# Half of the first feed-forward layer by seven block products for eight, in a two-layer decoder trunk on one core

## The chip, the cores and the metric

The kernel runs on one core of one Trainium2 chip. The metric is the device time of one execution in microseconds (us), the median of three runs. The engines are TensorE (PE, with its weight loads as PEld), VectorE (DVE), ScalarE (ACT), GpSimd (POOL) and SyncE (SP, whose queue issues nearly all transfers).

## The reference

One sequence of 1024 tokens with 1024 features passes a convolution layer and an attention layer; each is followed by a feed-forward layer (FFN) with squared ReLU and by a gated per-layer embedding (PLE).

```python
def reference(x, p, ...):
    h = x
    for i in range(DEPTH):                       # 2
        hn = rmsnorm(h, mix_norm[i])
        if i < N_A_LAYERS:                       # layer 0: GLU, 31 taps, layernorm, SiLU, pw2
            h = h + conformer_conv(hn, ...)
        else:                                    # layer 1: 16 heads, forget gates, w_o
            k, v, c_bhs = shared_kv(h, kv_norm, w_kvf, b_f)
            h = h + fox_attention(hn, attn_w_q[0], attn_w_o[0], k, v, c_bhs)
        hn = rmsnorm(h, ffn_norm[i])
        h = h + jnp.square(jax.nn.relu(hn @ ffn_w1[i])) @ ffn_w2[i]     # 1024 -> 4096 -> 1024
        gate = jax.nn.sigmoid(rmsnorm(h, ple_norm[i]) @ ple_w_gate[i])
        h = h + gate * (p[i] @ ple_w_proj[i])
    return rmsnorm(h, final_norm)
```

## The kernel before

The residual stream lies transposed in SBUF, features on partitions: `hT[0]` and `hT[1]` hold 512 tokens each ("half 0" and "half 1"), as 8 tiles of 128x512. All dense products run as three fp32r matmuls for one of float32: weights and tokens are each split into a rounded high part and the rest (`split`: ACT casts `h`, DVE or POOL subtracts to get `l`), and `mm3` issues high x high, high x low and low x high.

**A panel.** `linear` walks over weight panels of 128x1024 (512 KB). `panel` allots `raw`, loads it (line 120), casts it to `wh` on ACT (line 111) and subtracts to `wl` on DVE, or on POOL for half 0 (line 112). There are three buffers each of `wh` and `wl`, and `raws` of `raw` (2 in the first layer's pools, 1 during attention, 2 in the last pools of the output product). A panel is 24 matmuls of 128x512 (8 k-tiles by 3); `evac` then drains the PSUM bank on DVE.

**First layer** (`first`). After the GLU products DVE computes the taps of half 0 (`yA`) and then of half 1 (`yB`, 8 x 31 operations). Under the taps of half 1, PE runs `pw2` and the whole FFN of half 0 (`ffn`, four chunks of 8 inner tiles: `fa` panels, then `fb` panels; chunk c and panel j of half h are named `fa0hcj` and `fb0hcj`). `ln_silu(yB, 1)` (tiles `acc_m1`, `cs_m1`, `acc_ln1`, `st_ln1`, `bc_ln1`, `x1h1`, `x1l1`) gives the operand of half 1's `pw2`. Then come half 1's FFN and `ple` (panels `gt`). A Tile scheduler orders every engine's queue by program order, priorities and buffers; the order is fixed when the kernel is built.

**Second FFN** (`ffn_both`). Here tokens (two halves) and weights (halves of 4 k-tiles) are treated as 2x2 blocks, and `seven` forms the 2x2 block product by seven products for eight, in the order 1, 2, 5, 6, 3, 7, 4. The token operands are sums and differences of normalised halves (`z0f`, `z1f`; split operands `xf1` to `xf7`); `tokens_first` makes products 1 and 2's, which need half 0 alone, `tokens_rest` the others. `weight` makes the weight operands (`wt`, `wa`) from raw blocks `rwa`. `ffn_in` (PSUM tiles `psa`) writes the activations' seven combinations to DRAM (`rd`), and `ffn_out` (`psb`) reads them back as `rx`. The output product `out_product` before it (`wo`, eight panels of 5 k-tiles per half, then eight of 3; panel j of half h is `wo0jh` or `wo5jh`) ends with half 1's eight 3-tile panels in pools of their own; there `tokens_first` is called ahead of it.

## Time and profile before

| | |
|---|---|
| Time, median of 3 runs | 2612.85 us (2611.65 to 2614.08) |
| The profiled execution | 2616.24 us, span of the trace 2614.5 us |
| PE busy | 2457.6 us, 94% of the span |
| DVE busy | 1778.6 us, 68% |
| ACT busy | 1078.3 us, 41% |
| POOL busy | 913.1 us, 35% |
| DMA moved | 278.14 MB |

Busy PE time includes matmuls at the lower clock level; the granted clock (in shares of full speed) stands beside the busy time of a stretch. The mean clock over the execution was 0.969. Names of tiles are those of the program, and L137 is line 137 of the kernel before; in the changed kernel all lines stand 4 or more further down.

### The profile page before, as it was taken

To read this page: it belongs to the slowest core of one execution; us is meant where nothing else is said; L and a number is where in the kernel's file an instruction comes from. 1 tells how busy PE (TensorE), PEld (TensorE's weight loads), DVE (VectorE), ACT (ScalarE), POOL (GpSimd) and SP (SyncE) were. 2 spreads that over 40 slices of the span, in tenths; PEclk is the share of its full clock that TensorE was granted. 3 is DMA by queue.
4 is the path that set the end of the run, shared out by engine and by line. 5 is a ranking of instruction groups with operands and counts; after the bars stand their busy time and mean duration, and the time that the engine had idled before them with its cause. 6 is when DMAs were issued, how large, how long until landed. Compare 5 with 4: busy or idle time off the path is not lost.

```text
span 2614.5 us, 31465 instructions
## 1 busy us (share of the span) xinstructions
PE 2457.6 (94%) x11672; PEld 2053.1 (79%) x11672; DVE 1778.6 (68%) x2723; ACT 1078.3 (41%) x1670; POOL 913.1 (35%) x747
## 2 busy tenths in 40 slices
...
GB/s 128 49 71 183 57 78 105 97 97 98 92 89 105 97 97 93 101 83 88 62 57 50 51 49 73 107 59 167 97 208 154 141 212 267 153 145 121 36 125 113
DMA packets 101145, 278.14 MB, mean 106 GB/s; under 512 B 9840, under 2 KB 15600, under 8 KB 99584
## 3 DMA queue, kind: packets, MB, share of 16 engines
...
q14 instruction: 61, 0.50, 0.1%
...
## 4 chain that ended last, share of the span: by engine, by line
PE 76%; DVE 14%; issue 3%; ACT 3%; POOL 2%; DMA 2%; DVEq 0%; SPq 0%; POOLq 0%; ACTq 0%
PE ps_fb L137 13%; PE ps_fa L137 12%; PE psb L137 9%; PE psa L137 8%; PE ps_gt L137 7%; PE ps_wo L137 3%; PE psq L137 3%; DVE ya L332 3%; PE psv L137 3%; PE pg L137 3%; PE psk L137 3%; PE pa L137 3%; PE po L1002 2%; PE t L1032 2%; PE ps_pw L137 2%
## 5 line engine op out<-in xcount | busy, mean ns | idle before, releaser
L137 PE MATMUL psb<-rx,wb 128*128 128x512 f32 x1344 | 308.3, 392 | 5.7 <-ACT wb L111 5.7
L137 PEld LDWEIGHTS psb<-rx,wb 128*128 128x128 f32 x1344 | 254.0, 189 | 59.5 <-ACT wb L111 6.1
L137 PE MATMUL psa<-xf,wa 128*128 128x512 f32 x1200 | 281.4, 396 | 16.8 <-DVE xf L112 5.5
L332 DVE SCALAR_TENSOR_TENSOR ya<-u,wdw,ya 128x512 f32<-128x512 f32 x420 | 284.2, 747 | 0.0
L137 PEld LDWEIGHTS psa<-xf,wa 128*128 128x128 f32 x1200 | 228.4, 191 | 68.2 <-DVE xf L112 6.6
L111 ACT CAST wh_fb<-raw_fb 128x1024 fp32r<-128x1024 f32 x64 | 67.2, 1053 | 213.3 <-PE ps_fb L137 134.3
L111 ACT CAST wh_fa<-raw_fa 128x1024 fp32r<-128x1024 f32 x64 | 67.3, 1052 | 205.8 <-PE ps_fa L137 114.5
L390 DVE TENSOR_TENSOR hT<-ps_fb,hT 128x512 f32<-128x512 f32 x64 | 44.1, 689 | 147.8 <-PE ps_fb L137 147.8
L984 POOL TENSOR_SCALAR pr<-pr,sm 128x896 f32<-128x896 f32 (+7 forms) x128 | 100.0, 783 | 99.9 <-DVE sm L983 93.7
L205 POOL TENSOR_TENSOR r_g<-ms_g,mhalf 128x4 f32<-128x4 f32 x4 | 5.3, 1327 | 368.2 <-DVE ms_g L203 368.2
L112 DVE TENSOR_TENSOR pt<-t,pt 128x512 fp32r<-128x512 f32 (+1 forms) x160 | 99.2, 634 | 48.6 <-ACT pt L111 47.5
L1002 PE MATMUL po<-pt,V 128*128 128x256 f32 x640 | 121.7, 306 | 10.3 <-ACT pt L111 8.4
L112 POOL TENSOR_TENSOR wb<-rwb,wb 128x1024 fp32r<-128x1024 f32 x32 | 87.2, 2734 | 95.9 <-ACT wb L111 86.6
L982 ACT ACTIVATE pr<-pr,sm 128x896 f32<-128x896 f32 (+7 forms) x128 | 99.3, 776 | 51.9 <-DVE sm L981 35.0
L976 DVE CUSTOM_DVE_ANT_0 pr<-s,pr 128x512 f32<-128x512 f32 (+2 forms) x192 | 103.5, 551 | 22.9 <-POOL pr L963 12.8
L962 POOL TENSOR_SCALAR pr<-cb,ctok 128x896 f32<-128x896 f32 (+7 forms) x128 | 104.9, 826 | 36.1 <-PE t L1032 30.5
L384 DVE SCALAR_TENSOR_TENSOR fa<-ps_fa,bs_f 128x512 f32<-128x512 f32 x64 | 43.8, 689 | 108.4 <-PE ps_fa L137 105.0
L111 ACT CAST pt<-t 128x512 fp32r<-128x512 f32 (+1 forms) x160 | 84.0, 539 | 74.3 <-PE t L1032 70.9
L112 POOL TENSOR_TENSOR wl_fb<-raw_fb,wh_fb 128x1024 fp32r<-128x1024 f32 x32 | 77.4, 2420 | 104.0 <-ACT wh_fb L111 104.0
L112 POOL TENSOR_TENSOR wl_fa<-raw_fa,wh_fa 128x1024 fp32r<-128x1024 f32 x32 | 79.1, 2474 | 90.8 <-ACT wh_fa L111 90.8
L112 DVE TENSOR_TENSOR rx<-rx 128x1024 fp32r<-128x1024 f32 x56 | 79.9, 1437 | 41.8 <-ACT rx L111 41.8
L1002 PEld LDWEIGHTS po<-pt,V 128*128 128x128 f32 x640 | 92.8, 196 | 18.7 <-ACT pt L111 12.4
...
## 6 DMA issues: line engine op xcount, KB each, us to landing
...
rd<-e SPq DMA_DIRECT2D x112, 256.0 KB, 2.5
rx<-rd SPq DMA_DIRECT2D x28, 1024.0 KB, 5.6
...
```

The source lines that it names most:

```text
L111: copy(h, src)
L112: sub.tensor_tensor(l, src, h.bitcast(F32), ALU.subtract)
L137: self.nc.tensor.matmul(ps, p[:, k, :], q[:, k, :], start=(start and k == k0 and n == 0), stop=(stop and k == kt - 1 and n == 2), skip_gro ...
L332: nc.vector.scalar_tensor_tensor(d, s(j), w(j), o, ALU.mult, ALU.add)
L384: nc.vector.scalar_tensor_tensor(t, ps, 0.0, s[h][1], ALU.max, ALU.mult)
L390: nc.vector.tensor_tensor(hT[h][:, j, :], ps, hT[h][:, j, :], ALU.add)
L962: nc.gpsimd.tensor_scalar(z, cb[:, 0:W], -1.0, self.ctok[:, i, n : n + 1], ALU.mult, ALU.add)
L976: nc.vector.tensor_tensor_reduce(zz, ps[:, 0 : hi - lo], zz, -1.0, 3.0e38, ALU.add, ALU.min, sm[:, m : m + 1])
L982: nc.scalar.activation(z, z, AF.Exp, bias=sm[:, 0:1], scale=-1.0, accum_out=sm[:, 2:3])
L984: nc.gpsimd.tensor_scalar(z, z, sm[:, 3:4], 1.0, ALU.mult, ALU.mult)
L1002: nc.tensor.matmul(po, V[:, j, n % 4, :], pt[:, q, c : c + 256], start=(j == 0 and q == 0), stop=(jp == u and jj == 1 and q == 1),)
L1032: nc.tensor.transpose(ps[:, c : c + P], pr[b][:, j * P : (j + 1) * P], self.ident)
```

## The change

The first FFN keeps its first two chunks (16 of 32 inner tiles) as plain panels, once for each half (`PLAIN = (0, 1)`). The other 16 inner tiles are done for all tokens by `ffn_both`, two inner tiles of each weight half at a time (`pair=False`: groups `psa00` to `psa03`, then `psb00` and `psb01`). For that:

- The residual of half 0 and of half 1 is stored to DRAM twice each (`keep`, 2 MB a time): before the plain chunks (`hp`), from which the token operands are made, and after them (`hq`), to which `ffn_out` adds.
- The first pools of `first` end after half 0's plain chunks. Half 1's `ln_silu`, `pw2` and plain chunks run in new pools with one `raw` buffer: `work_pools(c1, 4, 1, 3)`.
- `tokens_first` (from `hp[0]`) and the first part of `tokens_rest` (from `hp[1]`) are called around half 1's plain chunks.
- `ple` of the first layer gets pools of its own and walks over the halves one after the other (`apart=(1, 0)`), loading its weights twice.

In the second FFN, `tokens_first` is called during the output product, ahead of half 1's first eight panels, and the last eight panels' pools have one `raw` buffer: `work_pools(c3, 2, 1, 1)`. The pools of `ffn_both` are allotted from the other side of SBUF.

```diff
+PLAIN = (0, 1)
...
-        for c in range(NCH):
+        for c in chunks:
             r = {h: self.xpair(f"r{l}{c}", h) for h in halves}
...
-            self.linear(a["wf2"][l, c], KT, r, evac2, f"fb{tag}{c}", **kw)
+            self.linear(a["wf2"][c], KT, r, evac2, f"fb{tag}{c}", **kw)
+        return s
...
-    def tokens_first(self, hT, gain, name):
-
-        hd = self.dr.tile([NH, P, KT * HB], F32, name=f"hd_{name}")
-        self.nc.sync.dma_start(hd[0], hT[0].rearrange("p k t -> p (k t)"))
-        bc = self.stats(hT, 0, name)[1]
-        f = self.slot([P, 2, 4, HB], F32, f"z0{name}")
+    def keep(self, dst, hT):
+        self.nc.sync.dma_start(dst, hT.rearrange("p k t -> p (k t)"))
+
+    def tokens_first(self, src, bc, gain, name):
+
+        f = self.slot([P, KT, HB], F32, f"z0{name}")
+        src = self.fetch(f, src)
+        f = f.rearrange("p (i k) t -> p i k t", i=2)
         x = {}
         for p, i in ((1, 0), (2, 1)):
...
+    def fetch(self, f, src):
+        if len(src.shape) == 3:
+            return src
+        self.nc.sync.dma_start(f.rearrange("p k t -> p (k t)"), src)
+        return f
...
-    def ffn_both(self, l, first):
+    def ffn_both(self, l, x, hd, t0, n, w2, rest, pair):
...
-                load(0)
-                load(1)
...
-                self.ffn_in(l, (0, 1), raw, sp, x, rd, between)
-                for g in range(2, 8):
-                    load(g)
-                    self.ffn_in(l, (g,), raw, sp, x, rd)
+                gs = [(0, 1)] if pair else [(0,)]
+                gs += [(g,) for g in range(len(gs[0]), n // 2)]
+                for i, g in enumerate(gs):
+                    for j in g:
+                        load(j)
+                    self.ffn_in(l, g, raw, sp, x, rd, None if i else between)
...
             with tc.high_priority(offset=back + 3000):
                 self.pw2(hT, x1, 0)
-                self.ffn(hT, 0, (0,), sub=nc.gpsimd)
-            self.sqp, self.sqt = self.tp, "bc"
+                self.keep(hp[0], hT[0])
+                s0 = self.ffn(hT, 0, (0,), PLAIN, sub=nc.gpsimd)[0]
+                self.keep(hq[0], hT[0])
+        with ExitStack() as c1:
+            self.work_pools(c1, 4, 1, 3)
+            self.psum_pools(c1, 4)
+            self.sqt, self.sqp = "sq", self.pool(c1, "sq0", 3)
             x1 = self.ln_silu(yB, 1)
             self.pw2(hT, x1, 1)
-            self.sqt, self.sqp = "sq", self.pool(c1, "sq0", 3)
-            self.ffn(hT, 0, (1,))
-            self.ple(hT, 0, pj0)
-        return pj1
+            self.keep(hp[1], hT[1])
+            first = self.tokens_first(hp[0], s0[1], "ffn0", "f0")
+            s1 = self.ffn(hT, 0, (1,), PLAIN)[1]
+            self.keep(hq[1], hT[1])
+            late = self.tokens_rest(*first, hp[1], s1[1])
+        hT = self.ffn_both(0, first[0], hq, KT * len(PLAIN), FF // P // 2 - 4 * len(PLAIN), self.a["wf2s0"], lambda: late, False)
+        with ExitStack() as c1:
+            self.work_pools(c1, 5)
+            self.psum_pools(c1, 5)
+            self.sqt, self.sqp = "sq", self.pool(c1, "sq5", 3)
+            self.ple(hT, 0, pj0, (1, 0))
+        return hT, pj1
...
-                if k0 == 0 and h == 0:
+                if h == 0 and k0 == 0:
                     for p in range(KSPLIT, NP - 1):
                         self.load_o(od, p)
+                elif h == 0:
+                    with tc.high_priority(offset=1):
+                        self.keep(hf[0], self.hn[0])
+                        first = self.tokens_first(self.hn[0], self.stats(self.hn, 0, "f1")[1], "ffn1", "f1")
         with ExitStack() as c3:
-            self.work_pools(c3, 2)
+            self.work_pools(c3, 2, 1, 1)
             self.psum_pools(c3, 2)
             self.sqp = None
-            first = self.tokens_first(self.hn, "ffn1", "f1")
             for _ in self.out_product(KSPLIT, NP, (1,)):
                 pass
-        return first
+        return self.hn, hf, first
```

**First place: from half 0 to half 1 in the first layer.** On PE, the last matmuls of half 0's second chunk (panel `fb0017`) were followed by the third chunk's first panel, and half 1's layer norm stood far behind, inside the fourth chunk:

```order
L137 MATMUL ps_fb0017_0_3726<-r01h0_3206,wh_fb0017_3722 128x512
L137 MATMUL ps_fb0017_0_3726<-r01l0_3207,wh_fb0017_3722 128x512
L137 MATMUL ps_fb0017_0_3726<-r01h0_3206,wl_fb0017_3723 128x512
L137 MATMUL ps_fa0020_0_3760<-f00xh0_2603,wh_fa0020_3756 128x512
L137 MATMUL ps_fa0020_0_3760<-f00xl0_2604,wh_fa0020_3756 128x512
L137 MATMUL ps_fa0020_0_3760<-f00xh0_2603,wl_fa0020_3757 128x512
```

In the changed kernel the three small groups of half 1's layer norm (`cs_m1`, `st_ln1`, `bc_ln1`) and then its `pw2` stand right behind the same panel:

```order
L141 MATMUL ps_fb0017_0_3729<-r01h0_3209,wh_fb0017_3725 128x512
L141 MATMUL ps_fb0017_0_3729<-r01l0_3210,wh_fb0017_3725 128x512
L141 MATMUL ps_fb0017_0_3729<-r01h0_3209,wl_fb0017_3726 128x512
L353 MATMUL cs_m1_3783<-acc_m1_3775,meanm_75 128x512
L193 MATMUL st_ln1_3793<-meanm_75,acc_ln1_3794 128x1 x4
L162 MATMUL bc_ln1_3825<-ident_68,r_ln1_3823 128x128 x4
L141 MATMUL ps_pw210_1_3886<-x1h1_3862,wh_pw210_3882 128x512
L141 MATMUL ps_pw211_1_3918<-x1h1_3862,wh_pw211_3914 128x512
```

The two chunks that stood between the last `fb0017` matmul and the layer norm's first matmul have gone from there, and nothing stands in their place.

**Second place: DVE in half 1's last plain chunk.** This is the part of the queue around the panels `fb0110` to `fb0113`, the evacuations of their PSUM banks into `hT1` and the splits of their weights; before:

```order
L112 TENSOR_TENSOR r01l1_5812<-fa0161_6060,r01h1_5811 128x512
L384 SCALAR_TENSOR_TENSOR fa0171_6096<-ps_fa0117_1_6071,bs_f011_5263 128x512
L112 TENSOR_TENSOR wl_fb0112_6168<-raw_fb0112_6165,wh_fb0112_6167 128x1024
L112 TENSOR_TENSOR r01l1_5812<-fa0171_6096,r01h1_5811 128x512
L390 TENSOR_TENSOR hT1_92<-ps_fb0110_1_6107,hT1_92 128x512
L112 TENSOR_TENSOR wl_fb0113_6200<-raw_fb0113_6197,wh_fb0113_6199 128x1024
L390 TENSOR_TENSOR hT1_92<-ps_fb0111_1_6139,hT1_92 128x512
L112 TENSOR_TENSOR wl_fb0114_6232<-raw_fb0114_6229,wh_fb0114_6231 128x1024
L390 TENSOR_TENSOR hT1_92<-ps_fb0112_1_6171,hT1_92 128x512
L112 TENSOR_TENSOR wl_fb0115_6264<-raw_fb0115_6261,wh_fb0115_6263 128x1024
```

In the changed kernel, the second half's normalised tokens (`z1f0`), the differences with the first half's (`z0f0`) and the split `xf05` stand between the same rows:

```order
L116 TENSOR_TENSOR r01l1_4761<-fa0171_5045,r01h1_4760 128x512
L427 SCALAR_TENSOR_TENSOR z1f0_5308<-z1f0_5308,vec_66,bs_f011_4212 128x512 x8
L394 TENSOR_TENSOR hT1_92<-ps_fb0110_1_5056,hT1_92 128x512
L441 TENSOR_TENSOR z0f0_4137<-z1f0_5308,z0f0_4137 128x1024
L116 TENSOR_TENSOR wl_fb0112_5117<-raw_fb0112_5114,wh_fb0112_5116 128x1024
L441 TENSOR_TENSOR z0f0_4137<-z1f0_5308,z0f0_4137 128x1024
L394 TENSOR_TENSOR hT1_92<-ps_fb0111_1_5088,hT1_92 128x512
L441 TENSOR_TENSOR z1f0_5308<-z1f0_5308 128x1024
L116 TENSOR_TENSOR xf05_5316<-z0f0_4137,xf05_5316 128x1024
L441 TENSOR_TENSOR z1f0_5308<-z1f0_5308 128x1024
L116 TENSOR_TENSOR xf05_5316<-z0f0_4137,xf05_5316 128x1024
L116 TENSOR_TENSOR wl_fb0113_5149<-raw_fb0113_5146,wh_fb0113_5148 128x1024
```

Eight normalisations and four differences now stand ahead of splits of `fb` panels that they don't feed.

**Third place: SP at the end of the output product.** Here the loads of the last eight panels (`raw_wo501` and on) stood behind four loads of second-FFN weights (`rwa100` to `rwa103`, 512 KB each):

```order
L120 DMA raw_wo071_14940<-in_wo 128x640
L526 DMA rwa100_15195<-in_wf1 128x2x512
L526 DMA rwa101_15196<-in_wf1 128x2x512
L526 DMA rwa102_15197<-in_wf1 128x2x512
L526 DMA rwa103_15198<-in_wf1 128x2x512
L120 DMA raw_wo501_15042<-in_wo 128x384
L120 DMA raw_wo511_15059<-in_wo 128x384
```

In the changed kernel they stand behind eight such loads and the two halves of a store of `xf12` (1 MB each, `xd_f1`), the second of which waits for the last split of `tokens_first`:

```order
L124 DMA raw_wo071_15029<-in_wo 128x640
L541 DMA rwa11_15232<-in_wf1 128x2x512 x4
L480 DMA xd_f1_15345<-xf12_14863 128x2048
L541 DMA rwa100_15224<-in_wf1 128x2x512
L541 DMA rwa101_15225<-in_wf1 128x2x512
L541 DMA rwa102_15226<-in_wf1 128x2x512
L541 DMA rwa103_15227<-in_wf1 128x2x512
L481 DMA xd_f1_15345<-xf12_14863 128x2048
L124 DMA raw_wo501_15071<-in_wo 128x384
L124 DMA raw_wo511_15088<-in_wo 128x384
```

Four loads and 2 MB of stores moved ahead of `raw_wo501`; on DVE and ACT, too, the splits of `rwa10` and `rwa11` now stand ahead of `wl_wo501`.

## Rows read from the trace of the kernel before

**Rows 1.** Page, part 1: busy us, share of the span, instructions of each engine.

```profile
PE 2457.6 (94%) x11672; PEld 2053.1 (79%) x11672; DVE 1778.6 (68%) x2723; ACT 1078.3 (41%) x1670; POOL 913.1 (35%) x747
```

**Rows 2.** Stretches: length; busy (count) PE, PEld, DVE, ACT, POOL; clock; DMA share; GB/s.

```profile
419.00:506.70 87.70, 87.70 (x388) 72.67 (x387) 69.92 (x108) 26.44 (x33) 38.41 (x16) 1.00 0.29 99
...
1079.80:1168.90 89.10, 89.10 (x401) 73.70 (x399) 48.35 (x66) 25.11 (x38) 3.12 (x2) 1.00 0.22 73
1824.80:1859.20 34.40, 17.82 (x66) 13.89 (x65) 26.59 (x29) 15.22 (x21) 3.79 (x2) 0.72 0.34 138
2160.00:2210.00 50.00, 43.95 (x180) 35.17 (x179) 44.89 (x42) 21.06 (x23) 20.70 (x8) 0.93 0.82 290
2482.20:2501.90 19.70, 14.13 (x57) 12.12 (x56) 9.15 (x14) 7.86 (x11) 2.39 (x2) 0.65 0.27 94
```

**Rows 3.** Timeline of DVE, 243 to 277: start, busy, instruction, count, idle before.

```profile
243.38 0.69 DVE L344 TENSOR_TENSOR acc_m<-y 128x512 f32<-128x512 f32 x1
...
274.25 2.29 DVE L358 SCALAR_TENSOR_TENSOR y<-y,vec,lsg 128x512 f32<-128x512 f32 x3
276.45 0.69 DVE L112 TENSOR_TENSOR x1l<-y,x1h 128x512 fp32r<-128x512 f32 x1
```

**Rows 4.** Timeline of PE, 243 to 280 us.

```profile
251.19 2.05 PE L349 MATMUL cs_m<-acc_m,meanm 128*128 128x512 f32 x2 [7.39 <-DVE acc_m L346]
...
276.31 1.65 PE L137 MATMUL ps_pw<-x1h,wh_pw 128*128 128x512 f32 x3 [7.37 <-ACT x1h L111]
```

**Rows 5.** Timeline of DVE, 484 to 513 us.

```profile
506.69 0.69 DVE L390 TENSOR_TENSOR hT<-ps_fb,hT 128x512 f32<-128x512 f32 x1 [4.75 <-PE ps_fb L137]
```

**Rows 6.** The tile raw_fb, all its instructions: ns minimum/median/maximum.

```profile
L111 ACT CAST wh_fb<-raw_fb x64: 1039/1053/1056, 360.9 to 1063.5; 128x1024 fp32r<-128x1024 f32 x64
...
L112 DVE TENSOR_TENSOR wl_fb<-raw_fb,wh_fb x32: 1224/1226/1226, 763.5 to 1064.6; 128x1024 fp32r<-128x1024 f32 x32
...
DMA to landing us min/median/max: 3.3/3.5/4.9
```

**Rows 7.** Timeline of all engines, 728.9 to 730.5 us.

```profile
728.96 1.23 DVE L112 TENSOR_TENSOR wl_fa<-raw_fa,wh_fa 128x1024 fp32r<-128x1024 f32 x1
...
730.22 0.33 SPq L120 DMA_DIRECT2D raw_fa<-in_wf  x1
```

**Rows 8.** Groups by line of DVE, 1820 to 1900: busy, mean ns.

```profile
L422 DVE SCALAR_TENSOR_TENSOR z0f<-hTb,vec,bs_f 128x512 f32<-128x512 f32 x8 | 5.4, 743 | 0.0
L112 DVE TENSOR_TENSOR wa<-rwa,wa 128x1024 fp32r<-128x1024 f32 x4 | 4.8, 1219 | 0.0
L436 DVE TENSOR_TENSOR z0f<-z1f,z0f 128x1024 f32<-128x1024 f32 x4 | 4.8, 1215 | 0.0
```

**Rows 9.** DMA issues: count, KB each, median us to landing.

```profile
hd<-hT SPq DMA_DIRECT2D x2, 2048.0 KB, 8.1
...
raw_wo<-in_wo SPq DMA_DIRECT2D x16, 192.0 KB, 2.3
...
xd_f<-xf SPq DMA_DIRECT2D x2, 1024.0 KB, 6.4
```

**Rows 10.** Timeline of PE, 1803 to 1862 us.

```profile
1804.73 0.50 PE L137 MATMUL ps_wo<-xoh,wh_wo 128*128 128x512 f32 x1 [2.16 <-ACT wh_wo L111]
...
1824.57 0.39 PE L137 MATMUL ps_wo<-xoh,wl_wo 128*128 128x512 f32 x1
...
1832.97 12.06 PE L137 MATMUL psa<-xf,wa 128*128 128x512 f32 x44 [0.76 <-DVE xf L112]
...
1859.15 3.05 PE L137 MATMUL psa<-xf,wa 128*128 128x512 f32 x9
```

**Rows 11.** The tile raw_wo, all its instructions, both widths.

```profile
L111 ACT CAST wh_wo<-raw_wo x32: 495/614/736, 1721.4 to 1817.7; 128x640 fp32r<-128x640 f32 x16, 128x384 fp32r<-128x384 f32 x16
L112 DVE TENSOR_TENSOR wl_wo<-raw_wo,wh_wo x32: 548/685/1451, 1722.1 to 1818.6; 128x640 fp32r<-128x640 f32 x16, 128x384 fp32r<-128x384 f32 x16
```

**Rows 12.** Timeline of PE, 1176 to 1197 us.

```profile
1177.63 0.82 PE L137 MATMUL psv<-wh_wv,atxh 128*128 128x272 f32 x2 [8.73 <-ACT wh_wv L111]
```

More of the change, by code (lines that the diff above doesn't have):

```diff
@@ L83, in v, with pool @@
         return self.vec[:, o + k : o + k + 1]
-    def pool(self, ctx, name, bufs, space=None):
+    def pool(self, ctx, name, bufs, space=None, side=None):
         kw = {} if space is None else {"space": space}
+        if side is not None:
+            kw["side"] = side
         return ctx.enter_context(self.tc.tile_pool(name=name, bufs=bufs, reuse_waits="tile", **kw))
@@ L372, in pw2, with ffn @@
         self.linear(self.a["wpw2"], KT, {h: x1}, evac, f"pw2{h}", halves=(h,), sub=self.subs[h])
-    def ffn(self, hT, l, halves=(0, 1), sub=None):
+    def ffn(self, hT, l, halves, chunks, sub=None):
         nc = self.nc
@@ L500, in seven @@
                 between(p)
-    def ffn_both(self, l, first):
+    def ffn_both(self, l, x, hd, t0, n, w2, rest, pair):
         nc, a = self.nc, self.a
-        rd = self.dr.tile([8, 16, P, HB], F32, name=f"rd{l}")
+        rd = self.dr.tile([8, n, P, HB], F32, name=f"rd{l}")
         with ExitStack() as c:
@@ L510, in ffn_both @@
             self.sqp = None
-            sp = self.pool(c, f"sw{l}", 2)
-            wr = self.pool(c, f"wr{l}", 4)
-            hT, x, _, hd, gain, name = first
+            sp = self.pool(c, f"sw{l}", 2, side="right")
+            wr = self.pool(c, f"wr{l}", 4, side="right")
             with ExitStack() as c1:
@@ L555, in load_h @@
                     hT.append(t)
-                for c in range(4):
-                    self.ffn_out(l, c, hT, load_h, wr, wq, sp, rd)
+                for c in range(n // 4):
+                    self.ffn_out(l, c, hT, load_h, wr, wq, sp, rd, w2, c == n // 4 - 1)
         return hT
@@ L613, in ffn_in, with ffn_out @@
         self.seven(w, lambda p: x[p], 2 * len(gs), 4, f"a{l}{gs[0]}", done, between=between)
-    def ffn_out(self, l, c, hT, load_h, wr, wq, sp, rd):
+    def ffn_out(self, l, c, hT, load_h, wr, wq, sp, rd, w2, last):
         nc = self.nc
@@ L621, in ffn_out @@
                 raw = pool.tile([P, 2, HB], F32, name=f"rwb{l}{c}{b}{q}", tag=tag)
-                nc.sync.dma_start(raw, self.a["wf2s"][l, c, q, :, b].rearrange("p (n f) -> p n f", n=2))
+                nc.sync.dma_start(raw, w2[c, q, :, b].rearrange("p (n f) -> p n f", n=2))
                 raws[q].append(raw)
@@ L643, in done @@
             nc.vector.tensor_tensor(o, ps, o, ALU.add)
-        order = (1, 5, 6, 3, 7, 2, 4) if c == 3 else (1, 2, 5, 6, 3, 7, 4)
+        order = (1, 5, 6, 3, 7, 2, 4) if last else (1, 2, 5, 6, 3, 7, 4)
         self.seven(w, x, 4, 4, f"b{l}{c}", done, order)
@@ L793, in attention @@
             self.flush(0)
+            hf = self.dr.tile([NH, P, KT * HB], F32, name="hf")
             for k0, k1, h in ((0, KSPLIT, 0), (KSPLIT, NP, 0), (0, KSPLIT, 1)):
@@ L1050, in build, with rest @@
             hT = k.load_x()
-        pj1 = k.first(hT)
-        hT = k.ffn_both(1, k.attention(hT))
+        hT, pj1 = k.first(hT)
+        hT, hf, first = k.attention(hT)
+        def rest():
+            k.keep(hf[1], hT[1])
+            return k.tokens_rest(*first, hT[1], k.stats(hT, 1, "f1")[1])
+        hT = k.ffn_both(1, first[0], hf, 0, 16, a["wf2s1"], rest, True)
         with ExitStack() as c:
@@ L1066, in _panels, with _blocks @@
     ).reshape(m // width, P, kk // P * width)
+def _blocks(w):
+    c = w.shape[0] // D
+    return np.ascontiguousarray(
+        w.reshape(2, c, 4, P, 2, 2, 2, P).transpose(1, 5, 3, 4, 0, 6, 2, 7)
+    ).reshape(c, 2, P, 4, D)
 def _halves(x):
```

42 lines of the change are left out of this document (20 added, 22 removed).

## The prediction

> **What bounds the kernel now.** First the page: PE is busy 94% of the span, DVE 68%, ACT 41% [rows 1]. So what PE executes, plus the places where it waits, is the time. Then the stretches: in half 0's chunks PE is busy 87.70 of 87.70 us with 388 matmuls, 0.2266 us each at granted clock 1.00 [rows 2]; a panel of 24 is 5.44 us. The first layer's PLE is as full, 89.10 of 89.10 [rows 2]. PE loses time where a stage begins: 66, 180 and 57 instructions in 34.4, 50.0 and 19.7 us at the second FFN's seams [rows 2]. The change adds such seams to a stretch that now has none. So I count matmuls first, then price each seam.
>
> The sum is made against the profiled execution, 2616.24 us with a span of 2614.5; that is 3.4 us above the median of 2612.85, to which I add the difference, since the terms are differences of stretches.
>
> **1. Work removed.** Sixteen inner tiles cost 2 chunks x 2 products x 8 panels x 24 matmuls x 2 halves = 1536; seven for eight makes 1344. 192 x 0.2266 = **-43.5 us**. The queues of both kernels give the same, 11538 and 11346 matmuls of 128x512.
>
> **2. Half 0 to half 1.** Now half 1's taps are done by the end of chunk 1, and half 0's chunks 2 and 3 cover half 1's layer norm. With these gone, PE's queue goes from the last `fb0017` matmul (506.7 by the evacuation row) straight to `cs_m1` [rows 5], and DVE starts `acc_m1` only behind that evacuation. The trace has the same chain uncovered once, for half 0: from the first `acc_m` at 243.38 to the first `pw2` matmul at 276.31, 32.9 us [rows 3, 4]. For half 1 add the evacuation (0.7) and three `wl_pw2` splits that stand in the chain on DVE (3 x 1.23, [rows 6]), less two tap operations inside the old chain (1.5): about 35.5 us. PE's own part of it, the three small groups, is paid now too: `cs_m` alone took 2.05 us at the low clock after the wait [rows 4], and I take 3 us for all three at full clock. **+32.5** (30 to 36).
>
> **3. Start of half 1's `pw2`.** PE interleaves the first three panels, 72 matmuls or 16.3 us. The fourth's weight split stands on DVE behind the last five SiLU multiplications (2.29 for three) and seven `x1l` (0.69 each), eight normalisations of `z0f0` (0.743), four `xf` splits (1.22), two evacuations (1.5) and itself (1.23) [rows 3, 6, 8]: 22.2 us, and I add 2 for waits on ACT's casts and on the 2 MB load. 24 against 16.3: **+7.7** (2.7, if only the two evacuations at PE's end and the split are left, to 12).
>
> **4. One raw buffer in half 1.** A panel's load can be issued only when the subtraction of the panel before has read the buffer: 730.19, then the load at 730.22 [rows 7]. Per panel that is a landing of 3.5 us, a cast of 1.05, a subtraction of 1.23 and two hand-overs of 0.03 [rows 6]: 5.84 us against PE's 5.44. The three `wh`/`wl` buffers give a lead once; the rate stays. 36 panels (four of `pw2`, 32 of the chunks) x 0.40 = **+14.4**. Bounds: 0, if the landing is at its minimum of 3.3 and PE starts with a lead; 20, if a panel queues another 0.15 us behind evacuations. Whether the landing itself is exposed to PE, not only the excess, is rival D. There the Trainium skill, "DMA: Bandwidth & Descriptors", section "Rules for kernel authors", speaks against this change: issue a transfer early and wait for it late, so that its fixed cost overlaps with compute. This case's rows show the late issue [rows 7], but no stretch of panels under it.
>
> **5. Operands made in half 1's last chunk.** On DVE, eight normalisations (5.9), four differences (4.9) and two splits (2.4) stand ahead of `wl_fb0113`, four more differences (4.9) ahead of `wl_fb0114`: 18.1 us [rows 8]. With the raw buffer single, what delays a split delays all loads behind it. DVE has 5.84 - 1.23 - 0.69 = 3.9 us per panel to spare; over two and a half panels that takes 9.7 of the 18.1, leaving 8.4. The 2 MB stores (8.1 us landing, [rows 9]) share the DMA engines with the loads: 1 more. **+9.4** (0 to 12).
>
> **6. The new block product's seams.** From the input part to the output part of the present one (2160 to 2210), PE needs 180 x 0.2266 = 40.8 of 50 us: 9.2 lost [rows 2]. **+9.5** (5 to 12). At its start the last four `xf` splits and the first weights share DVE: **+3** (0 to 8).
>
> **7. Block product to gates.** The second layer's seam, 2482.2 to 2501.9, holds some 23 matmuls of the gate product, so 19.7 - 5.2 = 14.5 us go to statistics and waiting; its clock is 0.65 [rows 2]. In the first layer today the same step costs 2 us: the statistics' own matmuls, in a stretch that is busy 89.1 of 89.1 [rows 2]. **+12.4** (8 to 15).
>
> **8. Output product and second FFN.** SP works in order: `raw_wo501` now stands behind 2 MB of stores and eight weight loads. The second store waits for the last `xf12` split, and that stands behind `wl_wo071`, which PE needs from 1799.2 (the last 5-tile panel ends 2.16 before 1804.73, and lasts 15 x 0.2266; [rows 10]): near 1800. From then some 4 MB must pass; at the 290 GB/s of a full stretch [rows 2] that is 14.5 us. With the cast, and seven weight operations of 1.22 ahead on DVE [rows 8], `wl_wo501` is done near 1818 (1811 by DVE's operations alone, 1822 if the traffic is slower). Then one raw buffer makes each of seven panels 2.4 + 0.50 + 0.55 + 0.1 = 3.55 us [rows 9, 11], where PE needs 9 x 0.2266 = 2.04: the last split is near 1843 and the product ends near 1845, against 1824.8 now [rows 10]. In return the first block product's operands are ready. Today its 48 matmuls end at 1845.0, 20 us after, and the second product starts at 1859.15 [rows 10]: 14.1 us for half 1's statistics, whose squares ACT still takes behind the four copies of product 1. So: 1845 + 1 + 10.9 + 14.1 = 1871. **+12** (0, if the loads come early, to 17).
>
> **9. Attention's start.** PE waits 8.7 us for the first `wv` panels [rows 12], behind two stores of 2 MB; one now goes out earlier. **-4** (-5 to 0).
>
> Sum: -43.5 + 32.5 + 7.7 + 14.4 + 9.4 + 9.5 + 3 + 12.4 + 12 - 4 = **+53.4**, so 2612.85 + 53.4 = **2666 us**.
>
> **The rivals.** *A, other side: the split buffers hide every load.* The three `wh`/`wl` pairs keep PE fed, so terms 3, 4, 5, 8 and the start in 6 vanish, and in term 8 the early operands save what PE now loses between 1802.6 and 1859.15 beyond 72 matmuls of the panels (16.3), 48 of the block product (10.9) and the 14.1 us: 56.6 - 41.3 = 15.3 [rows 10]. -43.5 - 15.3 + 32.5 + 9.5 + 12.4 - 4 = -8.4, 2604 us. It decides at a raw-buffer period below 5.44 us; the rows give 5.84, and 5.64 with the minimum landing. 0.06.
>
> *B, DVE's queue sets half 1's pace.* If each split also waits for one evacuation of 0.69, the period is 6.5: 36 x 0.69 = +25, 2691 us. For it: evacuations and splits alternate in the second place's rows. Against it: an evacuation stands two panels ahead of the split behind it. 0.12.
>
> *C, half 1 stays PE-bound, but the seams and term 8 hold.* Terms 3 to 5 vanish (31.5): 2635 us. 0.08.
>
> *D, every landing is exposed.* 36 x 3.5 = 126 in place of 14.4: 2778 us. Against it: the split buffers hold two panels in advance, so only the excess over 5.44 can show. 0.02.
>
> *E, terms cancel to no change.* Every term at its lower bound but 1 and 2: 0.02. That the change does not remove the work is excluded by the counts.
>
> **How the numbers follow.** My forecast has 0.70; its own range, from the bounds of terms 2 to 8 (the largest about 10 us to a side, together 17 when not all err one way), is 2645 to 2686. The whole range reaches to C below and B above: 2628 to 2693. 0.2% (5.2 us) is about what a measurement of this kernel can tell from no change; faster by more: 0.06 (A); within: 0.02 (E); slower: 0.92.
>
> **What would show it.** (2) PE idle some 35 us behind the last `fb0017` matmul, near 507 to 542, its clock low behind it. (3, 4) In half 1, `pw2` and `fa`/`fb` panels at 5.8 us, waits of PE ended by `wl` or `wh`, and each load issued right behind a `wl`. (5) A wait of several us near `fb0112` to `fb0114`. (6, 7) 10 us between `psa` and `psb` and some 14 between `psb` and `gt`, in the first layer too. (8) `ps_wo` of the last eight panels waiting on `raw_wo`, and product 2 starting 12 us later in relation to the output product's beginning. The prediction is wrong if half 1's panels stay at 5.44, or if PE finds work between 507 and 542.

## The result, and the profile after

The changed kernel takes 2670.3 us (median of 4 runs, 2668.6 to 2672.9) against 2613.3 for the kernel before in the same job: 1.022 times as long, 95% interval 1.0202 to 1.0237. 2666 was predicted. The profiled execution took 2671.5 us, its span is 2669.8, 55.3 above the span before.

The page's first part, which answers to [rows 1], shows that PE's busy share fell, and DVE's rose:

```profile
PE 2468.4 (92%) x11480; PEld 2018.3 (76%) x11480; DVE 1916.0 (72%) x2848; ACT 1104.0 (41%) x1688; POOL 956.1 (36%) x760
```

PE's busy time grew by 10.8 us though 192 matmuls are gone. The stretches of the changed kernel, in the order of the program, with the columns of [rows 2]: the gap behind half 0, half 1's `pw2`, its four plain products (`fa`, `fb`, `fa`, `fb`), the new block product, the gates, then the output product to the block product's second product, the second layer's block product, and its gates:

```profile
506.60:541.50 34.90, 6.20 (x20) 4.08 (x19) 25.77 (x38) 10.33 (x16) 1.01 (x1) 0.54 0.46 176
541.50:592.80 51.30, 48.06 (x192) 37.61 (x193) 37.86 (x52) 25.86 (x36) 0.00 (x0) 0.94 0.27 92
592.80:642.80 50.00, 48.08 (x210) 37.14 (x209) 20.99 (x27) 18.76 (x25) 1.01 (x1) 1.00 0.37 127
642.80:690.80 48.00, 46.15 (x193) 35.34 (x192) 15.12 (x18) 9.66 (x10) 0.00 (x0) 1.00 0.28 88
690.80:740.90 50.10, 46.50 (x193) 35.26 (x192) 18.62 (x23) 15.74 (x21) 0.00 (x0) 1.00 0.27 84
740.90:795.90 55.00, 48.10 (x194) 36.47 (x193) 31.96 (x36) 11.39 (x14) 0.00 (x0) 0.97 0.29 105
795.90:1117.90 322.00, 318.58 (x1347) 254.78 (x1345) 235.87 (x235) 130.08 (x158) 120.65 (x44) 0.99 0.47 168
1117.90:1209.80 91.90, 91.13 (x417) 75.34 (x415) 62.09 (x85) 35.30 (x52) 3.94 (x3) 1.00 0.42 144
1759.40:1905.60 146.20, 120.51 (x546) 96.15 (x546) 86.06 (x132) 51.75 (x85) 13.26 (x13) 0.93 0.38 131
1905.60:2546.40 640.80, 626.93 (x2642) 501.19 (x2641) 446.45 (x455) 235.60 (x280) 246.61 (x89) 0.98 0.43 150
2546.40:2639.40 93.00, 90.94 (x416) 75.57 (x416) 52.41 (x70) 30.24 (x41) 2.02 (x2) 1.00 0.34 115
```

The kernel before: half 0's last two chunks, half 1's `pw2`, its first two chunks and its last two, then the last three of the list above.

```profile
506.60:683.50 176.90, 176.90 (x788) 146.42 (x787) 77.74 (x85) 60.65 (x79) 73.59 (x31) 1.00 0.28 94
683.50:728.00 44.50, 44.00 (x194) 35.84 (x193) 31.05 (x42) 22.46 (x33) 0.00 (x0) 1.00 0.33 107
728.00:904.00 176.00, 176.00 (x786) 146.04 (x785) 72.89 (x83) 54.82 (x70) 1.01 (x1) 1.00 0.29 96
904.00:1079.80 175.80, 175.80 (x785) 145.85 (x784) 89.82 (x109) 69.20 (x94) 1.38 (x1) 1.00 0.29 98
1722.10:1859.20 137.10, 118.33 (x543) 97.48 (x543) 85.65 (x130) 50.25 (x84) 13.23 (x13) 0.92 0.39 140
1859.20:2482.20 623.00, 606.60 (x2642) 499.05 (x2641) 441.25 (x453) 232.88 (x276) 248.74 (x89) 0.99 0.44 153
2482.20:2584.00 101.80, 96.22 (x417) 79.80 (x416) 55.05 (x72) 33.45 (x44) 2.39 (x2) 0.93 0.33 111
```

Step by step, predicted and measured (differences of these stretches; the first, 34.9 us, less the 3 us that I take for the layer norm's own matmuls, which stood in half 0's chunks before; the new block product's 322.0 against the chunks that it replaces, 176.9 - 3 + 175.8 = 349.7; attention by the ends of its neighbours, 549.6 against 553.2):

| Step | Predicted | Measured |
|---|---|---|
| 2 half 0 to half 1 | +32.5 | +31.9 |
| 3 `pw2` of half 1 | +7.7 | +6.8 |
| 4 and 5, plain panels of half 1 | +23.8 | +27.1 |
| 1 and 6, block product for plain | -31.0 | -27.7 |
| 7 block product to gates | +12.4 | +2.8 |
| 9 attention's start and the rest of it | -4 | -3.6 |
| 8 output product to second product | +12 | +9.1 |
| second layer's block product | 0 | +17.8 |
| second layer's gates | 0 | -8.8 |
| **sum** | **+53.4** | **+55.4** |

The sum meets the spans' difference of 55.3. Two rows that were to be nothing, and step 7, went wrong by 9 to 18 us each and nearly cancelled.

**The seam of half 0 and half 1** in the changed kernel, PE's timeline, as [rows 4] showed it for half 0:

```profile
513.51 2.08 PE L353 MATMUL cs_m<-acc_m,meanm 128*128 128x512 f32 x2 [6.75 <-DVE acc_m L350]
528.83 1.86 PE L193 MATMUL st_ln<-meanm,acc_ln 128*128 128x1 f32 x8 [13.24 <-DVE acc_ln L201]
532.03 2.08 PE L162 MATMUL bc_ln<-ident,r_ln 128*128 128x128 f32 x8 [1.34 <-POOL r_ln L209]
541.48 1.65 PE L141 MATMUL ps_pw<-x1h,wh_pw 128*128 128x512 f32 x3 [7.37 <-ACT x1h L115]
```

It is the chain of [rows 3, 4]: from PE's last panel to `pw2` 34.9 us, of which PE is busy 6.2, at a granted clock of 0.54. The waits at its ends are about as long as for half 0 (6.75 for 7.39, and 7.37). The long one in the middle grew from 10.44 to 13.24: three `wl_pw` splits stand in the chain on DVE, as predicted, two of them here. In the kernel before, for half 0, it was this:

```profile
263.68 1.84 PE L189 MATMUL st_ln<-meanm,acc_ln 128*128 128x1 f32 x8 [10.44 <-DVE acc_ln L197]
```

**One raw buffer.** In half 1's second chunk, DVE's timeline shows each weight split waiting for ACT's cast, and the cast for the load:

```profile
704.27 1.23 DVE L116 TENSOR_TENSOR wl_fa<-raw_fa,wh_fa 128x1024 fp32r<-128x1024 f32 x1 [6.05 <-ACT wh_fa L115]
...
710.07 1.23 DVE L116 TENSOR_TENSOR wl_fa<-raw_fa,wh_fa 128x1024 fp32r<-128x1024 f32 x1 [3.32 <-ACT wh_fa L115]
...
716.15 1.22 DVE L116 TENSOR_TENSOR wl_fa<-raw_fa,wh_fa 128x1024 fp32r<-128x1024 f32 x1 [3.61 <-ACT wh_fa L115]
...
721.92 1.23 DVE L116 TENSOR_TENSOR wl_fa<-raw_fa,wh_fa 128x1024 fp32r<-128x1024 f32 x1 [3.30 <-ACT wh_fa L115]
...
727.77 1.23 DVE L116 TENSOR_TENSOR wl_fa<-raw_fa,wh_fa 128x1024 fp32r<-128x1024 f32 x1 [3.37 <-ACT wh_fa L115]
...
734.52 1.23 DVE L116 TENSOR_TENSOR wl_fa<-raw_fa,wh_fa 128x1024 fp32r<-128x1024 f32 x1 [4.27 <-ACT wh_fa L115]
```

The splits are 5.80, 6.08, 5.77, 5.85 and 6.75 us apart, PE needs 5.44. DVE is idle before each of them, so it is not DVE's own queue that delays them. Over the 24 panels of the first three products, which take 50.0, 48.0 and 50.1 us, the mean is 6.17 us a panel. The 24 loads issued from 587.7 to 729.0 landed after 3.75 us on the mean (median 3.55, longest 5.44); with 1.05 for the cast, 1.23 for the subtraction and the hand-overs that makes 6.1. And where the token operands stand in the queue, a little later:

```profile
746.38 1.23 DVE L116 TENSOR_TENSOR wl_fb<-raw_fb,wh_fb 128x1024 fp32r<-128x1024 f32 x1 [3.41 <-ACT wh_fb L115]
...
750.18 5.39 DVE L427 SCALAR_TENSOR_TENSOR z1f<-z1f,vec,bs_f 128x512 f32<-128x512 f32 x8 [1.93 <-DMA z1f<-hp]
...
757.22 1.22 DVE L116 TENSOR_TENSOR wl_fb<-raw_fb,wh_fb 128x1024 fp32r<-128x1024 f32 x1
...
764.63 1.22 DVE L116 TENSOR_TENSOR wl_fb<-raw_fb,wh_fb 128x1024 fp32r<-128x1024 f32 x1
```

From the split at 746.38 to the next at 757.22 it is 10.8 us: a wait of 1.9 us for the load of `z1f`, its eight normalisations (5.39 us) and a difference stand between; the next split of a weight follows after 7.4.

### The profile page after: what moved, and what is told of

Its sections match the earlier page's. It is cut to its first block, busy times and chain, and to the rows that moved or that the text cites. A ratio compares the mean times of both kernels' runs of the same rounds, so it can differ in the third digit from the quotient of the medians.

```text
span 2669.8 us, 31349 instructions
## 1 busy us (share of the span) xinstructions
PE 2468.4 (92%) x11480; PEld 2018.3 (76%) x11480; DVE 1916.0 (72%) x2848; ACT 1104.0 (41%) x1688; POOL 956.1 (36%) x760
## 4 chain that ended last, share of the span: by engine, by line
PE 64%; DVE 18%; DMA 8%; ACT 4%; issue 3%; POOL 3%; SPq 0%; ACTq 0%; DVEq 0%; POOLq 0%
PE psa L141 15%; PE psb L141 15%; PE ps_gt L141 7%; PE ps_fb L141 3%; DVE ya L336 3%; PE psv L141 3%; PE pg L141 3%; PE pa L141 3%; PE psq L141 3%; PE ps_wo L141 3%; PE psk L141 2%; DMA raw_fa<-in_wf 2%; PE po L1033 2%; PE t L1063 2%; PE ps_fa L141 2%
## 5 line engine op out<-in xcount | busy, mean ns | idle before, releaser
L141 PE MATMUL psb<-rx,wb 128*128 128x512 f32 x2016 | 480.5, 400 | 8.7 <-ACT wb L115 7.1
L141 PEld LDWEIGHTS psb<-rx,wb 128*128 128x128 f32 x2016 | 383.3, 190 | 105.0 <-ACT wb L115 8.4
L141 PE MATMUL psa<-xf,wa 128*128 128x512 f32 x1800 | 429.1, 399 | 8.6 <-POOL wa L116 5.0
L141 PEld LDWEIGHTS psa<-xf,wa 128*128 128x128 f32 x1800 | 341.1, 190 | 93.6 <-POOL wa L116 5.5
L116 POOL TENSOR_TENSOR wa<-wt,wa 128x1024 fp32r<-128x1024 f32 x18 | 52.4, 2914 | 463.3 <-ACT wa L115 447.0
L655 DVE TENSOR_TENSOR hTc<-psb,hTc 128x512 f32<-128x512 f32 x168 | 114.0, 684 | 62.9 <-PE psb L141 62.9
L115 ACT CAST rx<-rx 128x1024 fp32r<-128x1024 f32 x84 | 84.0, 1048 | 165.0 <-DMA rx<-rd 165.0
L116 POOL TENSOR_TENSOR wb<-wu,wb 128x1024 fp32r<-128x1024 f32 x36 | 104.9, 2916 | 99.7 <-ACT wb L115 99.7
L116 POOL TENSOR_TENSOR wa<-rwa,wa 128x1024 fp32r<-128x1024 f32 x33 | 82.4, 2499 | 132.6 <-ACT wa L115 132.6
L1013 ACT ACTIVATE pr<-pr,sm 128x896 f32<-128x896 f32 (+7 forms) x128 | 99.3, 776 | 53.2 <-DVE sm L1012 34.9
L1063 PE MATMUL t<-ident,pr 128*128 128x128 f32 x576 | 99.0, 282 | 7.9 <-DVE pt L116 4.6
L1033 PEld LDWEIGHTS po<-pt,V 128*128 128x128 f32 x640 | 92.7, 196 | 17.6 <-ACT pt L115 10.5
```

Source lines behind the costliest of these rows:

```text
L115: copy(h, src)
L116: sub.tensor_tensor(l, src, h.bitcast(F32), ALU.subtract)
L141: self.nc.tensor.matmul(ps, p[:, k, :], q[:, k, :], start=(start and k == k0 and n == 0), stop=(stop and k == kt - 1 and n == 2), skip_gro ...
L655: nc.vector.tensor_tensor(o, ps, o, ALU.add)
L1013: nc.scalar.activation(z, z, AF.Exp, bias=sm[:, 0:1], scale=-1.0, accum_out=sm[:, 2:3])
L1033: nc.tensor.matmul(po, V[:, j, n % 4, :], pt[:, q, c : c + 256], start=(j == 0 and q == 0), stop=(jp == u and jj == 1 and q == 1),)
```

## The experiments

### What slows the block products

A stretch of the input part without a wait, in the changed kernel:

```profile
796.00:947.00 151.00, 151.00 (x647) 121.37 (x646) 104.62 (x104) 58.13 (x74) 43.10 (x17) 1.00 0.57 206
```

647 matmuls in 151.0 us are 0.2334 each, where 388 took 87.70 before, 0.2260 [rows 2], at the same granted clock of 1.00. In 50 us of such a stretch the profile has 222 matmul records before and 215 or 216 after; below, the first is called full pace and the second slow. What differs is where the weights lie. In the built program the weight tiles (`wa`, `wb`) start at byte 149120 of each partition before, and at 204768 after: with `side="right"` the pools are laid down from the end of SBUF, and the end is no round number.

**Padding of 32 bytes** in front of the weights' pool, which then starts at a multiple of 64:

```diff
+            pad = self.pool(c, f"pad{l}", 1, side="right")
+            pad.tile([P, 8], F32, name=f"pad{l}")
             sp = self.pool(c, f"sw{l}", 2, side="right")
```

> The changed kernel with 32 bytes of padding at the end of SBUF, so that the weight tiles of both block products start at a multiple of 64 bytes; every queue keeps its order. Theory (address): in the changed kernel a matmul of the block products takes some 7 ns more (215 records in 50 us against 222) because its weights lie at 32 modulo 64; 4032 matmuls x 0.007 = 28 us less, about 2642 us, and 222 records in 50 us again. Rival (place or traffic): the slower pace comes from the other end of SBUF or from what the other engines do meanwhile; then nothing changes, 2670 us.

2669.3 us, 1.0219 (1.0199 to 1.0239) times the kernel before: no change, and 216 records in 50 us. So a multiple of 64 does not do, or the address is not it.

**The kernel before, moved by 32 bytes** (the same two lines, without `side`, ahead of its pool):

> The kernel before with its block product's pools moved by 32 bytes. Theory (address): 2688 matmuls x 0.007 = 19 us more, about 2632 us, with 215 records in 50 us in the block product and nothing slower elsewhere. Rival (place or traffic): no change, 2613 us.

2626.1 us, 1.0043 (1.0026 to 1.0060): slower, and 216 records in 50 us through both parts of its block product. Only the block product's own pools (weights, raw blocks, temporaries) lie elsewhere; the token operands do not, and every engine's queue is the same until the block product ends (around the step to the second layer's gates the order differs a little). So the address changes the pace. The two parts took 5 and 7 us more (308.5 against 303.5, 317.8 against 310.5); the rest of the 19 was hidden by waits that shrank.

**Padding of 96 bytes** (`[P, 24]`):

> The changed kernel with 96 bytes of padding at the end of SBUF instead of 32: the block products' weight tiles then start at 204672, a multiple of 128; every queue keeps its order. Theory (address, 128 bytes): weights that start at a multiple of 128 are at full pace (149120 in the kernel before), those at 32, 64 or 96 beyond one are not (149152, 204736, 204768); 222 records in 50 us again and 4032 x 0.007 = 28 us less, about 2642 us. Rival (place): weights at that end of SBUF are slower wherever they start; 215 records, 2670 us.

2652.2 us, 1.0137 (1.0119 to 1.0155): 18 us of the changed kernel's time are gone. The same stretch of matmuls, with the same queues:

```profile
797.50:944.00 146.50, 146.50 (x648) 121.34 (x647) 103.82 (x102) 58.04 (x74) 44.85 (x17) 1.00 0.59 211
```

648 in 146.5 us, 0.2261: full pace. The first block product ended 7.6 us sooner after its start, the second 17.9; gates and seams gave some of it back.

**The kernel before, moved by 128 bytes** (`[P, 32]`):

> The kernel before with its block product's pools moved by 128 bytes instead of 32; the queues are those of the run with 32. Theory (a multiple of 128 is enough): full pace, 222 records in 50 us, no change from the kernel before. Rival (any move costs, or the address needs a coarser multiple): slower by some 11 us, as with 32.

2626.5 us, 1.0043 (1.0028 to 1.0058), and 216 records in 50 us:

```profile
2270.00:2320.00 50.00, 50.00 (x216) 40.23 (x215) 33.87 (x38) 17.80 (x18) 28.87 (x10) 1.00 0.45 146
```

So a multiple of 128 is not the rule either. All six starts together:

| Weights start at byte | its remainder by 256 | pace |
|---|---|---|
| 149120 (before) | 128 | full |
| 204672 (96 bytes of padding) | 128 | full |
| 149152 (before, moved by 32) | 160 | slow |
| 204736 (32 bytes of padding) | 192 | slow |
| 204768 (changed kernel) | 224 | slow |
| 149248 (before, moved by 128) | 0 | slow |

The token operands (`xf`, `rx`) start at 9856 plus multiples of 16384 in all of them, a remainder of 128. Whether the weights need that remainder as such, or the tokens' remainder, none of these runs tells apart. A neighbouring product gives a hint: in attention's `psv` the streamed operand of 128x272 starts at remainders of 128, 192 and 0, while the loaded 128x128 operand stays at 128. In the kernel before, the median step from one such matmul to the next is 125.5, 124 and 126 ns, so there the two need not agree. That points to the loaded operand's own remainder; for 128x512 it is not shown.

### Half 1

**Two raw buffers**, and squares in the other temporaries to make room:

```diff
-            self.work_pools(c1, 4, 1, 3)
+            self.work_pools(c1, 4, 2, 3)
...
-            self.sqt, self.sqp = "sq", self.pool(c1, "sq0", 3)
+            self.sqp = None
```

> The changed kernel with two raw buffers in half 1's pools; to make room, squares take the same buffers as other temporaries. Theory (terms 4 and 5): panels come back to 5.44 us, and the delays of the last chunk are partly absorbed: 20 to 27 us less, about 2647 us. Rival (DVE's queue sets half 1's pace): the splits are as late as before, less than 5 us gained.

2631.1 us, 1.0063 (1.0048 to 1.0078): 39 us gained (43.5 between the profiled executions), more than either theory gave. Half 1's four plain products run without a wait:

```profile
576.00:751.80 175.80, 175.80 (x785) 145.84 (x784) 86.22 (x99) 53.53 (x68) 1.01 (x1) 1.00 0.33 108
```

175.8 us against 203.1, as in the kernel before. `pw2` took 46.1 us for 51.3. The rest, 11.5 us, is that `pw2` began at 529.96 and not at 541.48: the layer norm now starts under chunk 1. In the built program the one buffer fewer had moved the temporaries 4 KB down: `acc_m1` lies where half 0's `wl_fb0016` was, which PE reads until 501.2, and in the order as built its first sum stands behind the last evacuation, at 507.4. With two raw buffers the temporaries lie on half 0's temporaries, which are free sooner, and the sums are under way at 471.

**One raw buffer, but the temporaries in that place** (a gap of 4 KB ahead of their pool, squares as in the run above):

```diff
+            gap = self.pool(c1, "gap", 1)
+            gap.tile([P, T], F32, name="gap")
             self.tt = self.pool(c1, "tt4", 3)
```

> The changed kernel, still with one raw buffer in half 1, but with 4 KB left free behind the weight buffers, so that the temporaries do not lie on the last weight buffer of half 0's pools; squares take temporaries, as in the run with two raw buffers. Theory (place of the temporaries): half 1's layer norm starts under chunk 1 as in that run, pw2 begins near 530 and not 541.5, and the panels of half 1 stay at 5.8 us: about 2658 us. Rival (the raw buffer does both): pw2 begins at 541 as before, 2670 us.

2664.8 us, 1.0187 (1.0171 to 1.0203). `pw2` begins here:

```profile
529.25 1.65 PE L141 MATMUL ps_pw<-x1h,wh_pw 128*128 128x512 f32 x3 [7.37 <-ACT x1h L115]
```

12 us sooner, so the place of the temporaries makes that part (5.5 us are left of it in the median). The squares moved in both runs, too, but the sums that begin the chain need none of them. The four plain products take 205.9 us, from 580.4 to 786.3, so the pace is the raw buffer's: the two runs differ by 34 us.

**The layer norm called inside the first pools:**

```diff
                 self.keep(hq[0], hT[0])
+            self.sqp, self.sqt = self.tp, "bc"
+            x1 = self.ln_silu(yB, 1)
         with ExitStack() as c1:
...
-            x1 = self.ln_silu(yB, 1)
```

> The changed kernel with half 1's layer norm called inside the first pools, so that it may start when the taps end (488.8) and not behind the last evacuation (507.4). Theory (term 2): the 33 us chain then overlaps with chunk 1's last panels; its end moves 15 to 18 us forward, about 2654 us. Rival: the chain waits for buffers that chunk 1 holds and ends as late as now, 2670 us.

2682.0 us, 1.0258 (1.0243 to 1.0273): 12 us slower, on neither theory's side. `pw2` began at 531.2, 10 us sooner, but took 61.6 us for 51.3: DVE's new order puts splits of block product weights and the normalisations of `z0f` between the last `x1l`, and PE waited 9.6 us for `x1h` and 6.6 for `x1l`. The block product began at 797.2 (795.9 in the changed kernel). Most of the rest was lost in attention, 557.1 us from the gates' end to the first `ps_wo` for 549.6, where the scheduler's order had changed as well; why is open.

### The steps to the gates

**Pools of the block products on the same side as all others:**

```diff
-            sp = self.pool(c, f"sw{l}", 2, side="right")
-            wr = self.pool(c, f"wr{l}", 4, side="right")
+            sp = self.pool(c, f"sw{l}", 2)
+            wr = self.pool(c, f"wr{l}", 4)
```

> The changed kernel with the block products' pools allotted from the same side as all others; their weights then start at 149120, as before. Theory (address, and the side sets when the gate's weights can load): pace as before, 28 us less, but 9 us more at each of the two steps to the gate product, whose buffers again lie on the block product's, and up to 10 more at the first layer's block product's start: 2660 to 2670 us. Rival (the seam is cheap for another reason): only the pace changes, about 2642 us.

2669.1 us, 1.0202 (1.0181 to 1.0222): no gain, at full pace. PE at the first layer's step, first in this run, then in the changed kernel:

```profile
1115.41 0.94 PE L193 MATMUL st_g<-meanm,acc_g 128*128 128x1 f32 x8
1122.77 0.80 PE L141 MATMUL ps_gt<-g0xh,wh_gt 128*128 128x512 f32 x1 [6.42 <-ACT wh_gt L115]
...
1123.79 1.92 PE L162 MATMUL bc_g<-ident,r_g 128*128 128x128 f32 x8
1125.51 1.71 PE L193 MATMUL st_g<-meanm,acc_g 128*128 128x1 f32 x8
```

```profile
1117.86 0.95 PE L193 MATMUL st_g<-meanm,acc_g 128*128 128x1 f32 x8
1118.66 0.48 PE L141 MATMUL ps_gt<-g0xh,wh_gt 128*128 128x512 f32 x1
...
1125.38 1.16 PE L162 MATMUL bc_g<-ident,r_g 128*128 128x128 f32 x8 [0.76 <-POOL r_g L209]
```

On the same side, the first gate matmul waits 6.42 us for its cast weights, whose buffers lie on those of the block product; the statistics and broadcasts behind it run at the lower clock level (granted clock 0.50 from 1122.7 to 1130.0). On the other side it follows the statistics at once. From the last block product to the end of the gates it is 101.1 us here and 91.9 there, 89.1 before [rows 2]: the predicted 12.4 of step 7 is 12.0 with the old side and 2.8 with the new. The second layer shows the same, 101.2 against 93.0. These two kernels also differ in pace. The run with 96 bytes of padding has the new side at the full pace of this run: 92.7 and 95.5 us, so the side by itself, with the order that comes with it, is worth 8.4 and 5.7 us. That is why next to nothing is gained here in all: the two block products take 24 us less than in the changed kernel (316.4 for 322.0 and, from the second product on, 622.5 for 640.8), the two steps 17.4 more, and the first block product begins 3.3 us later.

**The kernel before with its block product on the other side** (same three pool lines as in the run with 96 bytes of padding):

> The kernel before with the block product's pools at the other end of SBUF, as in the changed kernel, but with weights at a multiple of 128 bytes. Theory (term 7's miss): the gate product's weight buffers no longer lie on the block product's, so its first panels load before the last product ends; the step to the gate product, which cost 14.5 us, costs some 6, and the kernel 8 to 9 us less, about 2606 us. Rival: the step is cheaper in the changed kernel for another reason, and nothing changes here.

2611.9 us, 0.9994 (0.9984 to 1.0003): not told from no change. In its profile the step takes 96.7 us for 101.8:

```profile
2482.60:2579.30 96.70, 93.80 (x416) 77.87 (x416) 53.28 (x71) 31.36 (x42) 2.39 (x2) 0.96 0.35 112
```

5 us, not 9, and they hardly show in the medians. At full pace the step is dearer: in the changed kernel, too, it took 95.5 us with 96 bytes of padding for 93.0 without. I take it that a slower last product leaves the other engines further ahead. The kernel before moved by 32 bytes points the same way (97.2 us for 101.8, with the old side), but its queues differ at this step; it was not tried by itself.

### The output product

**The first operands made where they were before**, in pools with two raw buffers:

```diff
-                elif h == 0:
-                    with tc.high_priority(offset=1):
-                        self.keep(hf[0], self.hn[0])
-                        first = self.tokens_first(self.hn[0], ...)
...
-            self.work_pools(c3, 2, 1, 1)
+            self.work_pools(c3, 2)
...
+            self.keep(hf[0], self.hn[0])
+            first = self.tokens_first(self.hn[0], ...)
```

> The changed kernel with the second FFN's first operands made where they were made before, behind the output product's first panels of half 1, and two raw buffers for the last eight panels. Theory (term 8): from the output product's first matmul to the block product's second product took 146.2 us, before the change 137.1; with the old place 9 us come back, about 2661 us. Rival: the early operands pay for the late panels, and it is 2670 us or more.

2662.8 us, 1.0179 (1.0163 to 1.0195): 7.4 us gained, and from the first `ps_wo` to the second product 135.7 us, below the 137.1 before. In the changed kernel SP's queue and the casts on ACT show the step as it was predicted:

```profile
1834.72 0.34 SPq L480 DMA_DIRECT2D xd_f<-xf  x1
1835.10 3.21 SPq L541 DMA_DIRECT2D rwa<-in_wf  x4
1840.85 0.34 SPq L481 DMA_DIRECT2D xd_f<-xf  x1
1841.23 33.79 SPq L124 DMA_DIRECT2D raw_wo<-in_wo  x8
```

```profile
1850.33 0.51 ACT L115 CAST wh_wo<-raw_wo 128x384 fp32r<-128x384 f32 x1 [6.18 <-DMA raw_wo<-in_wo]
1855.66 0.51 ACT L115 CAST wh_wo<-raw_wo 128x384 fp32r<-128x384 f32 x1 [4.82 <-DMA raw_wo<-in_wo]
1859.28 0.51 ACT L115 CAST wh_wo<-raw_wo 128x384 fp32r<-128x384 f32 x1 [3.11 <-DMA raw_wo<-in_wo]
1862.85 0.51 ACT L115 CAST wh_wo<-raw_wo 128x384 fp32r<-128x384 f32 x1 [3.06 <-DMA raw_wo<-in_wo]
```

The store at 1840.85 waits for the last `xf12` split, the first `raw_wo` goes out behind it at 1841.23 and lands 9 us later; then one panel follows another every 3.6 us, where PE needs 2.04.

### Mended together

**Three mends**: 96 bytes of padding, two raw buffers in half 1, and `work_pools(c3, 2, 2, 1)`, with the early operands kept:

> The changed kernel with three mends: weights of the block products at a multiple of 128 bytes, two raw buffers in half 1 (squares in the temporaries), and two raw buffers also for the output product's last eight panels, whose loads stay at their late place in SP's queue. Theory: 39 us from half 1 and 18 from the alignment, as measured apart, and from term 8 the part that is the single buffer's: a panel 2.04 to 2.5 us instead of 3.57 for seven panels, 7 to 11 us. 2670 - 39 - 18 - 9 = 2604 us. Rival: the late place alone makes term 8, and the second buffer gives under 3 us: 2611 us.

2596.8 us, 0.9931 (0.9916 to 0.9946): 0.7% faster than the kernel before. From the first `ps_wo` to the second product:

```profile
1707.50:1844.10 136.60, 117.72 (x545) 97.25 (x546) 85.72 (x132) 51.67 (x85) 13.26 (x13) 0.92 0.42 140
```

136.6 us for 146.2: the second buffer takes 9.6 us off. That is as good as before, but not because the late place in SP's queue is free. PE's waits for cast panels around the output product's end (us in total, times, longest), first in the changed kernel, then in this run:

```profile
PE ps_wo L141 <- ACT wh_wo L115: 11.6, 7, 5.7
```

```profile
PE ps_wo L141 <- ACT wh_wo L115: 5.6, 1, 5.6
```

From its first matmul to the start of its last, the output product takes 102.5 us before, 120.4 in the changed kernel and 111.2 here: 9.2 us go with the single buffer, and 8.7 stay with the late place. The early operands pay for those: from there to the second product it is 34.6 us before, 25.8 in the changed kernel and 25.4 here.

**Two of them, and the old order instead of the third:**

> The changed kernel with the block products' weights at a multiple of 128 bytes, two raw buffers in half 1 and the second FFN's first operands made where they were made before. Theory: the parts add, 2670 - 39 - 18 - 9 = 2604 us, some 11 us below the kernel before in the same job. Rival: the parts share waits and add to less, 2615 us or more, no better than the kernel before.

2599.8 us, 0.9938 (0.9925 to 0.9951): the parts add, with 4 us to spare.

## Why the prediction was right

The time lies 4 us above the forecast, and the mechanism held in most of its steps; the closeness of the sum is partly luck.

- **Step 2** held in place and size: 34.9 us without a panel on PE against 35.5, low clock in it. What the prediction did not see is why DVE starts only behind the last evacuation. I put it down to the queue's order; the order comes from the temporaries' place on one of half 0's last weight buffers, and 11.5 us of the 32 go with that place.
- **Steps 3 to 5** held as a mechanism and in their sum: 33.9 us against 31.5, and the second buffer gave 34 us. But term 4 was too small: 24 panels without token operands took 148.1 us for 132.0 before, 16.1 more where 0.40 a panel gives 9.6. It used the median landing of 3.5 us; with one buffer the mean counts, 3.75 here, since nothing laid by takes up a late landing. Terms 3 and 5, a little too large, made up for most of it. The 6.17 us a panel lie as near to rival B's 6.5 as to the forecast's 5.84, but B's mechanism was not it: DVE is idle ahead of each split, waiting for the cast. Rival D, the landing fully exposed, would have been near 9 us a panel, since the whole load adds to 5.44. The Trainium skill's advice to issue a load early and wait late ("DMA: Bandwidth & Descriptors", section "Rules for kernel authors") agrees in direction; what was lost here is the excess over PE's time alone.
- **Steps 1 and 6**: a gain of 27.7 for 31.0. 192 matmuls less were worth 43.5 only at full pace: 1344 matmuls at 0.2334 instead of 0.2260 cost 9.9. (The row's quotient, 87.70 by 388, is 0.2260 and not the 0.2266 of the prediction, which changes term 1 by 0.1.) The seams took 322.0 - 313.7 = 8.3 us, not 12.5.
- **Step 7** failed: 2.8 for 12.4. The size came from the second layer's step, whose gate weights wait for the block product's buffers; the new side of SBUF frees them. I had costed `side="right"` at nothing without asking what lay on what. At equal pace the side is worth 8.4 us at the first layer's step and 5.1 to 5.7 at the second's; the rest of the 8.8 us by which the second layer's step got shorter goes with the slow pace (93.0 us slow, 95.5 full).
- **A step was missing**: the pace of 2688 matmuls in the second layer, 17.8 us, and of 1344 in the first. No row of before could show it, since there all weights of such matmuls start at a remainder of 128.
- **Step 8** held: 9.1 for 12, with the order of events as described, and in its parts: the output product ended 17.9 us later (20 forecast), 9.2 of them by the single buffer and 8.7 by the late place in SP's queue, and the early operands gave 8.8 back (8 forecast).
- **Step 9** held in size, 3.6 for 4, but the wait that it names fell by 1.8 us only (6.92 for 8.73); two waits of PE for the statistics of attention's input, 1.9 and 0.9 us, went as well.
- **Rival A** needed a period below 5.44; with the second buffer the panels do run without a wait, and the kernel, with the pace mended, ends 18.7 us below the one before. The change's idea pays; what cost it was where its buffers lie and how many they are.
